# Two heads' compressed probabilities turned in one transpose, placed last in an unbroken run of five

## The chip, the cores and the metric

The kernel runs on one core of a Trainium2 chip. The metric is device time in microseconds (us) from start to end of the program. The core has a matrix engine, TensorE (PE), and four others that work beside it: VectorE (DVE), ScalarE (ACT), GpSimd (POOL), and SyncE (SP), whose queue starts most DMA transfers. Each engine works through its own list of instructions in order and waits on semaphores for the others. Matrix results go to PSUM, in banks of 128 partitions by 512 fp32 columns; operands are read from SBUF.

## The reference

One step of a hybrid decoder layer: a normalised and modulated input, one wide projection, two token mixers (sparse attention and a gated DeltaNet), a merge, an output projection and an MLP. The change touches the sparse attention of the 512 prompt tokens. Its three branches each have their own softmax, and each is scaled by a gate per head before the sum:

```python
s = jnp.einsum('nqghd,ncgd->nqghc', q, kc) * scale
p_cmp = _masked_softmax(s, (kc_end[None, :] <= qp)[None, :, None, None, :])
o_cmp = jnp.einsum('nqghc,ncgd->nqghd', p_cmp, vc)
...
out = gates[..., 0:1] * o_cmp + gates[..., 1:2] * o_slc + gates[..., 2:3] * o_win
```

`kc` and `vc` are keys and values compressed over blocks of tokens; with 512 tokens there are 31 of them, padded to 32. There are 16 query heads in four groups that share keys and values.

## The kernel before

All matrix work in fp32 precision is done as split products: a value is written as a rounded part (hi, type fp32r) and a remainder (lo), and hi x hi, lo x hi and hi x lo are summed in PSUM. So most things that TensorE reads are made by a pair: ACT copies a rounded hi, DVE subtracts it to give lo.

`attention` goes over 32 units (g, i, pr): four groups g, two pairs of heads pr in each, and four blocks of 128 queries i. For each unit `scores` makes probabilities, and `values`, one unit later, multiplies them with the values, so that scores of one unit and values of the one before overlap. In `scores` each of the two heads gets three arrays: `p0` for the 32 compressed keys, `p1` for the selected blocks and `p2` for the window, both 128*(i+1) wide. TensorE makes the scores (tiles `bsp<-K,qst` in the profile), DVE adds the mask and finds the extreme (L1440), ACT takes the exponential and the row sum (L1464), DVE turns sums and gates into one factor per array (L1469 to L1474), and POOL multiplies the six arrays by their factors (L1477), in the order p0, p1, p2 of the first head, then of the second. The two `p0` lie next to each other in one buffer of `pcs` (a part of `consts` in the profile), 64 columns in all.

In `values` probabilities must be turned, so that keys lie on partitions. `tr` (L160) is a TensorE transpose against the identity. The two `p0` are turned first, one after the other, each into 32 partitions of a PSUM bank `pct`; ACT copies them as the rounded part into `st` (L1486, rows 0 to 31) and DVE puts the remainder into rows 32 to 63 (L1487). `st` is the tile `msk`, shown as `rounded`. Then `flipped(j)` turns block j of `p1` and `p2` of both heads, four transposes into a bank `pt`; ACT makes `pth` from it (L1495) and DVE `ptl` (L1496). The products are collected in a bank `po` (`bek` in the profile); the one with the compressed values reads `vcp`, which holds the same 32 rows of compressed values at partitions 0 to 31 and 32 to 63, hi and lo side by side in its columns:

```python
mm(po[:, 0:256], vcp[:, g], st, start=False, stop=False)
```

The banks of `scores`, `pct` and `pt` come from one ring of four PSUM banks (`bsp`).

Around this, `run` weaves the other generators and a stream of projection units together (`bpg` in the profile: eight times three matmuls for each half of the tokens, L153). The Python code keeps an estimate of TensorE's time, `pe_time`, and lets a generator go on when it is due; `yield` names how long it may rest. The emission order and a priority for attention then go to a scheduler that lays down each engine's list. Units of the stream may have a gate; the `ma` units are gated on `split_q`, which attention itself reaches only every fourth unit. A helper, `quarters`, already had the form that the change takes over: first instruction at normal priority, the following ones at priority 20000 and kept in program order, so that they stand together.

Of the kernel before, what the change touches and what calls it, by code (L numbers as in the profile page):

```python
# [11 lines left out]
ALU = mybir.AluOpType  # L12
# [44 lines left out]
def f32(x):  # L57
    return x.bitcast(F32)
# [11 lines left out]
def hybrid_step(ctx: ExitStack, tc: tile.TileContext, A, O, dbg=None):  # L70


    nc = tc.nc
# [27 lines left out]
    def t2(name, dt=F32):  # L101
        return wk.tile([128, SLOT], dt, name=name, tag="t2k")
# [14 lines left out]
    def cst(shape, dt):  # L117

        n = 1
        for v in shape[1:]:  # L120
            n *= v
        r = dt == F32R
        x = (rounded if r else consts)[0:shape[0], cused[r]:cused[r] + n]
        cused[r] += -(-n // 8) * 8
        assert cused[r] <= (CW, CR)[r]
        x = x.bitcast(dt) if dt == I32 else x
        return x if len(shape) == 2 else x.rearrange("p (a b) -> p a b", a=shape[1])
# [12 lines left out]
    def bank(tag):  # L140
        tag = "sp" if tag in ("sc", "pt") else tag
        return ps.tile([128, 512], F32, name="b" + tag, tag=tag, bufs=4 if tag == "sp" else 2)
# [7 lines left out]
    pe_time = [0.0]  # L150
# [8 lines left out]
    def tr(out, in_, idn):  # L159
        nc.tensor.transpose(out, in_, idn)  # L160
        pe_time[0] += 0.107
# [17 lines left out]
    for hf in range(2):  # L179
        c = slice(hf * 512, hf * 512 + 512)  # L180
# [32 lines left out]
    ident = cst([128, 128], F32)  # L213
# [15 lines left out]
    pc = bank("pt")  # L229
# [1193 lines left out]
    def scores(g, i, pr):  # L1423
        n = 128 * (i + 1)
        cs = slice(i * 128, (i + 1) * 128)
        mk, mc = slot["mk"], slot["mc"]
        mx = wk.tile([128, 6], F32, name="mx", tag="sm6", bufs=12)
        sm = wk.tile([128, 6], F32, name="sm", tag="sm6", bufs=12)
        pcs.append(pcs.pop(0))
        pc = pcs[-1]  # L1430
        pp = []

        def score(q, K, c0, c1):
            p = bank("sc")
            mm(p[:, 0:c1 - c0], q[0][:, cs], K[:, g, c0:c1], start=True, stop=False)
            mm(p[:, 0:c1 - c0], q[1][:, cs], K[:, g, c0:c1], start=False, stop=True)
            return p

        def maskmin(out, p, m, acc, init=3.0e38):
            nc.vector.tensor_tensor_reduce(out=out, in0=p, in1=m, scale=1.0, scalar=init, op0=ALU.add, op1=ALU.min, accum_out=acc)  # L1440

        for a_ in range(2):
            ql = qst[2 * g + pr][a_]
            a = a_ * 3
            p0 = pc[:, a_]
            x = t2("ps")
            p1, p2 = x[:, 0:n], x[:, n:2 * n] if i < 2 else t2("pw")[:, 0:n]
            if i < 3:
                pb = score(ql, slot["Ks"], 0, 32 + n)
                maskmin(p0, pb[:, 0:32], mc[:, i], mx[:, a:a + 1])  # L1450
                maskmin(p1, pb[:, 32:32 + n], mk[:, 512 - n:512], mx[:, a + 1:a + 2])
            else:
                pb = score(ql, slot["Ks"], 0, 288)
                maskmin(p0, pb[:, 0:32], mc[:, i], mx[:, a:a + 1])
                maskmin(p1[:, 0:256], pb[:, 32:288], mk[:, 0:256], mx[:, a + 1:a + 2])
                yield 0.3 * YA
                pb = score(ql, slot["Ks"], 288, 544)
                maskmin(p1[:, 256:512], pb[:, 0:256], mk[:, 256:512], mx[:, a + 1:a + 2], mx[:, a + 1:a + 2])
            yield 0.3 * YA
            pd = score(ql, slot["Kw"], 0, n)  # L1460
            maskmin(p2, pd[:, 0:n], mk[:, 512 - n:512], mx[:, a + 2:a + 3])
            parts = (p0, p1, p2)
            for b_, x in enumerate(parts):
                nc.scalar.activation(x, x, AF.Exp, scale=-1.0, bias=mx[:, a + b_:a + b_ + 1],  # L1464
                                     accum_out=sm[:, a + b_:a + b_ + 1])
            pp.append(parts)
            yield 0.5 * YA
        sc = wk.tile([128, 6], F32, name="scl", tag="sm6", bufs=12)
        nc.vector.tensor_scalar(sm, sm, 1.0e-30, None, op0=ALU.max)  # L1469
        nc.vector.reciprocal(sc, sm)  # L1470
        h0 = 16 + (g * 4 + pr * 2) * 3
        nc.vector.tensor_tensor(sc, sc, gtok[:, i, h0:h0 + 6], op=ALU.mult)
        if i == 0:
            nc.vector.tensor_scalar(sc[:, 0:4:3], sc[:, 0:4:3], rv, None, op0=ALU.mult)  # L1474
        for a_ in range(2):
            for b_, x in enumerate(pp[a_]):
                nc.gpsimd.tensor_scalar(x, x, sc[:, a_ * 3 + b_:a_ * 3 + b_ + 1], 1.0, op0=ALU.mult, op1=ALU.mult)  # L1477
        return pp

    def values(g, i, pr, pp):  # L1480
        cs = slice(i * 128, (i + 1) * 128)
        pct = bank("pt")
        for a_ in range(2):
            tr(pct[0:32, a_ * 128:(a_ + 1) * 128], pp[a_][0], ident)
        st = msk.rearrange("p a c -> p (a c)")
        nc.scalar.copy(out=st[0:32], in_=pct[0:32, 0:256])  # L1486
        nc.vector.tensor_tensor(st[32:64], pct[0:32, 0:256], f32(st[0:32]), op=ALU.subtract)  # L1487

        def flipped(j):
            pt = bank("pt")  # L1490
            for b_ in range(2):
                for a_ in range(2):
                    tr(pt[:, (b_ * 2 + a_) * 128:(b_ * 2 + a_ + 1) * 128], pp[a_][1 + b_][:, j * 128:(j + 1) * 128], ident)
            hi, lo = t2("pth", F32R)[:, 0:512], t2("ptl", F32R)[:, 0:512]
            nc.scalar.copy(out=hi, in_=pt)  # L1495
            nc.vector.tensor_tensor(lo, pt, f32(hi), op=ALU.subtract)  # L1496
            return hi, lo
        ptt = flipped(0)
        yield 1 * YA
        po = bank("ek")  # L1500
        for j in range(i + 1):
            for n in range(4):
                mm(po[:, 0:256], slot["V2"][:, n // 2, j, g], ptt[n % 2][:, (n // 2) * 256:(n // 2) * 256 + 256],
                   start=(n + j == 0), stop=(n == 3 and j == i))
                if n + j == 0:
                    mm(po[:, 0:256], vcp[:, g], st, start=False, stop=False)
            if j < i:
                ptt = flipped(j + 1)
                yield 1 * YA
        tm = pp[0][1][:, 0:128]  # L1510
        for a_ in range(2):
            r = slice(a_ * 64, a_ * 64 + 64)
            nc.scalar.copy(out=tm[r], in_=po[64:128, a_ * 128:(a_ + 1) * 128])
            nc.vector.tensor_tensor(tm[r], po[0:64, a_ * 128:(a_ + 1) * 128], tm[r], op=ALU.add)
        t = tma[:, g * 2 + pr, cs]
        nc.vector.scalar_tensor_tensor(t, t, 1.0, tm, op0=ALU.add, op1=ALU.mult)
# [483 lines left out]
```

## Time and profile before

| what | value |
|---|---|
| timed runs | 1309.7, 1305.91 and 1313.38 us, median 1309.7 |
| the profiled execution | 1307.84 us |
| its span, first to last instruction | 1306.1 us |
| mean granted TensorE clock | 0.969 of full |
| busy: PE, DVE, ACT, POOL | 1216.6, 843.8, 647.2, 230.1 us |
| first and last copy of line L1486 | 523.2 and 876.2 us |

Busy time counts instructions that run; matmuls overlap their neighbours, so that the time from one start to the next is less than the duration of one. The granted clock is the share of full speed that TensorE was allowed. The chain of work is followed back from the last instruction to whatever released each step. A wait is put down to the semaphore that came last.

### The profile page before, as it was taken

Reading aid. Unit: us, or ns where it says so; the run is one execution under the profiler, and the core shown is the slowest. Engines: PE = TensorE matmul, PEld = TensorE weight load, DVE = VectorE, ACT = ScalarE, POOL = GpSimd, SP = SyncE. Lnnn points to the kernel's source line nnn. Section 1 sums busy time; section 2 is a strip of 40 time slices with the busy share of each in tenths; the row PEclk is TensorE's granted clock in tenths of the full one; section 3 lists DMA queues with packets and bytes.
Section 4 is the critical chain, followed back from the end, with each engine's and each line's share of the span. In section 5 each row is a group of like instructions: output and inputs, shape, how many; then the busy total and the mean of one; then the engine's idle time right before and its main releaser. Section 6 shows DMA issues by size and latency. Waiting matters only on the chain. (4 is left out here: it accounts for less than half of the span.)

```text
span 1306.1 us, 26716 instructions
## 1 busy us (share of the span) xinstructions
PE 1216.6 (93%) x10356; PEld 1150.1 (88%) x10356; DVE 843.8 (65%) x2291; ACT 647.2 (50%) x1561; POOL 230.1 (18%) x323
## 2 busy tenths in 40 slices
PE   4899899999888999799998899999999999999997
PEld 3788889989788999678887798989999999999996
DVE  4576958795357788787777787896834334334355
ACT  4565857654243336656646677574643132232244
POOL 2112100112111111312221323230431021020000
PEclk9899989999699999899999899999999999999999
DMA  8852412425613345346344222371732332332533
GB/s 273 216 156 74 126 32 51 119 78 151 182 47 108 103 130 146 98 116 197 99 116 136 74 72 85 94 196 33 210 95 69 98 95 83 97 97 83 161 90 105
DMA packets 234834, 149.82 MB, mean 115 GB/s; under 512 B 9290, under 2 KB 230018, under 8 KB 234444
## 3 DMA queue, kind: packets, MB, share of 16 engines
q1 hardware_dynamic: 224804, 134.77, 36.4%
q0 software_dynamic: 2240, 6.38, 1.8%
q10 hardware_dynamic: 7664, 6.97, 1.8%
q8 instruction: 81, 1.33, 0.4%
q14 instruction: 45, 0.37, 0.1%
HBM read 136.87 MB, written 15.60 MB: 117 GB/s over the span
## 5 line engine op out<-in xcount | busy, mean ns | idle before, releaser
L153 PE MATMUL bpg<-hh,wh 128*128 128x256 f32 (+1 forms) x1168 | 342.2, 293 | 1.2 <-ACT hh L1521 0.7
L153 PE MATMUL bpg<-hh,wl 128*128 128x256 f32 (+1 forms) x1168 | 337.5, 289 | 2.0 <-DVE wl L401 2.0
L153 PE MATMUL bpg<-hl,wh 128*128 128x256 f32 (+1 forms) x1168 | 337.7, 289 | 0.0
L153 PEld LDWEIGHTS bpg<-hh,wh 128*128 128x128 f32 x1168 | 225.2, 193 | 5.2 <-issue 2.0
L153 PEld LDWEIGHTS bpg<-hh,wl 128*128 128x128 f32 x1168 | 224.5, 192 | 4.0 <-DVE wl L401 2.5
L153 PEld LDWEIGHTS bpg<-hl,wh 128*128 128x128 f32 x1168 | 225.5, 193 | 1.5 <-issue 0.8
L401 DVE TENSOR_TENSOR wl<-raw,wh 128x1024 fp32r<-128x1024 f32 x149 | 183.0, 1229 | 65.7 <-ACT wh L397 60.3
L397 ACT CAST wh<-raw 128x1024 fp32r<-128x1024 f32 x117 | 121.6, 1048 | 181.9 <-PE bpg L153 174.5
L153 PE MATMUL bpg<-act,wh 128*128 128x264 f32 (+1 forms) x1024 | 186.5, 284 | 0.0
L153 PEld LDWEIGHTS bpg<-act,wh 128*128 128x128 f32 x1024 | 157.7, 188 | 0.1
L153 PE MATMUL bpg<-act,wl 128*128 128x264 f32 (+1 forms) x512 | 145.0, 284 | 0.2 <-DVE wl L401 0.2
L153 PE MATMUL bpg<-h2h,wh 128*128 128x256 f32 (+1 forms) x448 | 126.7, 283 | 0.0
L153 PE MATMUL bpg<-h2h,wl 128*128 128x256 f32 (+1 forms) x448 | 126.6, 282 | 0.0
L153 PE MATMUL bpg<-h2l,wh 128*128 128x256 f32 (+1 forms) x448 | 126.3, 282 | 0.0
L1848 POOL TENSOR_TENSOR r<-r 128x520 f32<-128x520 f32 (+2 forms) x40 | 54.1, 1354 | 291.2 <-ACT r L1847 291.2
L1811 DVE SCALAR_TENSOR_TENSOR o_dn<-bpg,consts,o_dn 128x256 f32<-128x256 f32 x80 | 38.3, 484 | 100.3 <-PE bpg L153 100.3
L153 PEld LDWEIGHTS bpg<-act,wl 128*128 128x128 f32 x512 | 96.5, 189 | 0.5 <-DVE wl L401 0.4
L153 PEld LDWEIGHTS bpg<-h2h,wl 128*128 128x128 f32 x448 | 84.4, 188 | 0.3 <-DVE wl L401 0.2
L153 PEld LDWEIGHTS bpg<-h2l,wh 128*128 128x128 f32 x448 | 84.4, 188 | 0.0
L153 PEld LDWEIGHTS bpg<-h2h,wh 128*128 128x128 f32 x448 | 84.3, 188 | 0.0
L153 PE MATMUL bsp<-K,qst 128*128 128x288 f32 (+6 forms) x288 | 68.9, 317 | 5.5 <-DVE consts L267 2.3
L1851 DVE TENSOR_TENSOR act<-r,act 128x520 fp32r<-128x520 f32 (+2 forms) x40 | 23.6, 590 | 73.4 <-ACT act L1850 73.3
(634 smaller groups left out, 2453.3 us busy)
## 6 DMA issues: line engine op xcount, KB each, us to landing
raw<-in_w_in SPq DMA_DIRECT2D x68, 512.0 KB
wa<-in_w_ada SPq DMA_DIRECT2D x48, 512.0 KB
raw<-in_w_down SPq DMA_DIRECT2D x40, 512.0 KB
raw<-in_w_up SPq DMA_DIRECT2D x36, 512.0 KB
raw<-in_w_out SPq DMA_DIRECT2D x12, 512.0 KB
Sx<-in_state_dn SPq DMA_DIRECT2D x16, 256.0 KB
out_s_dn<-Sx SPq DMA_DIRECT2D x16, 256.0 KB
pg<-in_cache_k_slc SPq DMA_DIRECT2D x16, 128.0 KB
```

The source lines that it names most:

```text
L153: nc.tensor.matmul(out, lhs, rhs, start=start, stop=stop)
L397: nc.scalar.copy(out=wh, in_=raw)
L401: nc.vector.tensor_tensor(wl[:, 0:kp], raw[:, 0:kp], f32(wh[:, 0:kp]), op=ALU.subtract)
L1811: nc.vector.scalar_tensor_tensor(xi[:, q], p[:, 0:n], mod[:, m + i, 0:1], xi[:, q], op0=ALU.mult, op1=ALU.add)
L1848: nc.gpsimd.tensor_tensor(r, r, r, op=ALU.mult)
L1851: nc.vector.tensor_tensor(b_, r, f32(a), op=ALU.subtract)
```

## The change

The two compressed blocks of a unit are no longer turned one by one. `scores` hands over the 64 columns that hold both, and one transpose turns them into 64 partitions, head 0 in rows 0 to 31 and head 1 in rows 32 to 63. Since the two heads now lie on different partitions, the rounded copy and the subtraction are done once per head, 32 rows by 128 columns each. For head 1 hi and lo change places in `st` (hi in rows 32 to 63, lo in 0 to 31), which `vcp` allows, since its two halves are equal.

The transposes also get a new order. Block 0 is turned first, beginning with the window part of the second head, which POOL scales last; the other three follow at high priority and in program order, and the compressed transpose comes after them as the fifth. For the following blocks the four stand together in the same way. On ACT and DVE the copies of the compressed part come after `pth` and `ptl`.

```diff
         for a_ in range(2):
             for b_, x in enumerate(pp[a_]):
                 nc.gpsimd.tensor_scalar(x, x, sc[:, a_ * 3 + b_:a_ * 3 + b_ + 1], 1.0, op0=ALU.mult, op1=ALU.mult)
+        pp.append(pc.rearrange("p a c -> p (a c)"))
         return pp
 
     def values(g, i, pr, pp):
         cs = slice(i * 128, (i + 1) * 128)
-        pct = bank("pt")
-        for a_ in range(2):
-            tr(pct[0:32, a_ * 128:(a_ + 1) * 128], pp[a_][0], ident)
         st = msk.rearrange("p a c -> p (a c)")
-        nc.scalar.copy(out=st[0:32], in_=pct[0:32, 0:256])
-        nc.vector.tensor_tensor(st[32:64], pct[0:32, 0:256], f32(st[0:32]), op=ALU.subtract)
+        lo_hi = (slice(0, 32), slice(32, 64))
+
+        def turn(out, in_, first):
+            with nullcontext() if first else tc.high_priority(20000):
+                r = nc.tensor.transpose(out, in_, ident)
+            if not first:
+                tc.keep_in_program_order(r)
+            pe_time[0] += 0.107
 
         def flipped(j):
             pt = bank("pt")
-            for b_ in range(2):
-                for a_ in range(2):
-                    tr(pt[:, (b_ * 2 + a_) * 128:(b_ * 2 + a_ + 1) * 128], pp[a_][1 + b_][:, j * 128:(j + 1) * 128], ident)
+            for a_ in (1, 0):
+                for b_ in (1, 0):
+                    turn(pt[:, (b_ * 2 + a_) * 128:(b_ * 2 + a_ + 1) * 128], pp[a_][1 + b_][:, j * 128:(j + 1) * 128], a_ + b_ == 2)
+            if j == 0:
+                pct = bank("pt")
+                turn(pct[0:64, 0:128], pp[2], False)
             hi, lo = t2("pth", F32R)[:, 0:512], t2("ptl", F32R)[:, 0:512]
             nc.scalar.copy(out=hi, in_=pt)
             nc.vector.tensor_tensor(lo, pt, f32(hi), op=ALU.subtract)
+            if j == 0:
+                for a_ in range(2):
+                    c = slice(a_ * 128, (a_ + 1) * 128)
+                    nc.scalar.copy(out=st[lo_hi[a_], c], in_=pct[lo_hi[a_], 0:128])
+                    nc.vector.tensor_tensor(st[lo_hi[1 - a_], c], pct[lo_hi[a_], 0:128], f32(st[lo_hi[a_], c]), op=ALU.subtract)
             return hi, lo
         ptt = flipped(0)
```

The lists below name tiles as the profile does: `bsp<-consts 32x128` and `bsp<-consts 64x128` are the compressed transposes before and now, `bsp<-consts,ps` and `bsp<-consts,pw` those of `p1` and `p2`, `bek<-pth`, `bek<-ptl` and `bek<-rounded` the products with the values, `bsp<-K,qst` scores. L160 and L153 are helpers; in the changed kernel the transposes of `values` have line L1488. TensorE's list has 384 of these transposes in 86 groups before and 352 in 70 groups now.

TensorE's list before, at the end of the third of the four stretches in which projection matmuls are missing (731 to 747 us of the trace):

```order
L153 MATMUL bek<-ptl,V_5790 128x256
L160 MATMUL bsp<-consts 32x128
L160 MATMUL bsp<-consts,ps 128x128 x3
L160 MATMUL bsp<-consts 32x128
L160 MATMUL bsp<-consts,ps 128x128 x2
L160 MATMUL bsp<-consts,pw 128x128 x2
L160 MATMUL bsp<-consts,ps 128x128
L160 MATMUL bsp<-consts,pw 128x128 x4
```

The same place now:

```order
L153 MATMUL bek<-ptl,V_5790 128x256
L1488 MATMUL bsp<-consts,pw 128x128
L1488 MATMUL bsp<-consts,ps 128x128
L1488 MATMUL bsp<-consts,pw 128x128
L1488 MATMUL bsp<-consts,ps 128x128
L1488 MATMUL bsp<-consts 64x128
L1488 MATMUL bsp<-consts,pw 128x128
L1488 MATMUL bsp<-consts,ps 128x128
```

The compressed transposes stood between the others, each where its head's arrays are; now one of them ends the run of block 0.

ACT's list before, at the first call of `values` (L1387 belongs to the sample's DeltaNet):

```order
L1464 ACTIVATE ps,sm<-ps,mx 128x128
L1486 CAST rounded<-bsp 32x256
L1464 ACTIVATE consts,sm<-consts,mx 128x32
L1464 ACTIVATE ps,sm<-ps,mx 128x128 x2
L1495 CAST pth<-bsp 128x512
L1387 CAST rounded<-bsp 8x128
```

And now:

```order
L1464 ACTIVATE ps,sm<-ps,mx 128x128
L1464 ACTIVATE consts,sm<-consts,mx 128x32
L1464 ACTIVATE ps,sm<-ps,mx 128x128 x2
L1502 CAST pth<-bsp 128x512
L1507 CAST rounded<-bsp 32x128
L1387 CAST rounded<-bsp 8x128
L1502 CAST pth<-bsp 128x512
L1507 CAST rounded<-bsp 32x128
```

The one copy ahead of `pth` has become two behind it, the second of them behind the next call's `pth`.

TensorE's list before, in the fourth of those stretches (ahead of and in 811 to 819 us; `bek<-consts,ma` belongs to the modulation):

```order
L153 MATMUL bek<-pth,V_5790 128x256
L153 MATMUL bsp<-K,qst 128x416 x2
L153 MATMUL bpg<-hl,wh 128x264
L153 MATMUL bek<-consts,ma 128x9 x2
L153 MATMUL bek<-ptl,V_5790 128x256
L153 MATMUL bek<-pth,V_5790 128x256
L153 MATMUL bek<-ptl,V_5790 128x256
L153 MATMUL bsp<-K,qst 128x384 x2
L153 MATMUL bpg<-hh,wl 128x264
L160 MATMUL bsp<-consts 32x128 x2
```

And now:

```order
L153 MATMUL bek<-pth,V_5790 128x256
L153 MATMUL bsp<-K,qst 128x416 x2
L153 MATMUL bek<-consts,ma 128x9 x2
L153 MATMUL bek<-ptl,V_5790 128x256
L153 MATMUL bek<-pth,V_5790 128x256
L153 MATMUL bek<-ptl,V_5790 128x256
L153 MATMUL bsp<-K,qst 128x384 x2
L1488 MATMUL bsp<-consts,ps 128x128 x4
L1488 MATMUL bsp<-consts 64x128
L153 MATMUL bsp<-K,qst 128x288 x2
```

The projection matmuls (`bpg`) that stood between the pieces of attention here now stand ahead of them.

## Rows read from the trace of the kernel before

**Rows 1.** The page's first part, busy time, share of the span and instructions.
```profile
PE 1216.6 (93%) x10356; PEld 1150.1 (88%) x10356; DVE 843.8 (65%) x2291; ACT 647.2 (50%) x1561; POOL 230.1 (18%) x323
```

**Rows 2.** Windows: length; busy per engine; then granted clock, DMA share, GB/s.
```profile
515.00:900.00 385.00, 355.64 (x2892) 322.04 (x2891) 299.53 (x1018) 239.06 (x713) 98.44 (x198) 0.97 0.39 113
531.00:547.00 16.00, 11.17 (x66) 7.91 (x65) 12.40 (x57) 13.55 (x42) 5.65 (x13) 0.77 0.32 98
687.00:703.00 16.00, 13.11 (x130) 11.24 (x123) 12.54 (x45) 8.80 (x28) 2.52 (x5) 1.00 0.59 182
731.00:747.00 16.00, 10.75 (x52) 8.67 (x52) 9.97 (x41) 12.69 (x39) 5.19 (x11) 0.70 0.33 88
811.00:819.00 8.00, 6.45 (x47) 5.30 (x48) 5.69 (x25) 4.53 (x18) 3.34 (x6) 0.81 0.97 246
```

**Rows 3.** The chain that ended last: start, length, engine, line.
```profile
946.57 303.91 PE bpg L153 x2529
...
1258.02 0.22 PE bsp L160 x2
```

**Rows 4.** Windows of 4 us in the third and the fourth stretch.
```profile
735.00:739.00 4.00, 2.30 (x10) 1.92 (x11) 3.88 (x13) 3.88 (x12) 0.00 (x0) 0.81 0.33 80
739.00:743.00 4.00, 2.34 (x9) 1.36 (x8) 3.58 (x18) 3.88 (x12) 2.25 (x5) 0.50 0.19 56
743.00:747.00 4.00, 3.82 (x17) 3.45 (x18) 1.41 (x6) 3.90 (x13) 2.94 (x7) 0.50 0.00 0
...
815.00:819.00 4.00, 3.17 (x16) 3.01 (x16) 1.78 (x4) 1.29 (x6) 2.88 (x5) 0.62 1.18 288
```

**Rows 5.** Line L160: count, ns min/median/max, first and last start, forms.
```profile
L160 PE MATMUL bsp<-consts,ps x208: 270/273/476, 523.0 to 882.4; 128*128 128x128 f32 x104
...
L160 PE MATMUL bsp<-consts x85: 164/272/396, 89.1 to 874.2; 128*32 128x128 f32 x64, 128*8 128x128 f32 x13, 128*88 128x128 f32 x3, 128*128 128x128 f32 x3
```

**Rows 6.** PE's timeline, a transpose among projection matmuls: start, duration, instruction.
```profile
703.43 0.28 PE L153 MATMUL bpg<-hh,wl 128*128 128x264 f32 x1
703.55 0.27 PE L160 MATMUL bsp<-consts,ps 128*128 128x128 f32 x1
...
703.78 0.28 PE L153 MATMUL bpg<-hl,wh 128*128 128x264 f32 x1
```

**Rows 7.** Windows of line L1486 alone: ACT busy and count.
```profile
531.00:547.00 16.00, 0.72 (x2) 0.77 0.32 98
...
811.00:819.00 8.00, 0.27 (x1) 0.81 0.97 246
```

**Rows 8.** Lines of the copies, columns as in rows 5.
```profile
L1486 ACT CAST rounded<-bsp x32: 344/361/363, 523.2 to 876.2; 32x256 fp32r<-32x256 f32 x32
...
L1487 DVE TENSOR_TENSOR rounded<-bsp,rounded x32: 412/414/415, 524.0 to 878.1; 32x256 fp32r<-32x256 f32 x32
...
L1387 ACT CAST rounded<-bsp x8: 236/248/255, 406.3 to 565.5; 8x128 fp32r<-8x128 f32 x8
...
L1389 DVE TENSOR_TENSOR rounded<-bsp,rounded x8: 279/280/280, 407.4 to 567.0; 8x128 fp32r<-8x128 f32 x8
...
L1495 ACT CAST pth<-bsp x80: 557/586/619, 524.7 to 883.3; 128x512 fp32r<-128x512 f32 x80
```

**Rows 9.** PE's waits from 515 to 900 us: total, times, longest.
```profile
PE bsp L160 <- POOL consts L1477: 4.3, 4, 2.2
...
PE bsp L153 <- DVE rounded L1487: 2.2, 2, 1.4
PE bsp L160 <- POOL ps L1477: 2.0, 4, 0.8
...
PE bsp L160 <- DVE rounded L1487: 0.7, 1, 0.7
```

**Rows 10.** POOL's timeline in the third stretch; in brackets idle before and releaser.
```profile
740.63 0.29 POOL L1477 TENSOR_SCALAR consts<-consts,scl 128x32 f32<-128x32 f32 x1 [11.89 <-DVE mx L1440]
```

**Rows 11.** Window of line L160 alone: PE and weight load busy, then clock, DMA.
```profile
591.00:607.00 16.00, 4.69 (x30) 3.45 (x30) 1.00 0.81 233
```

## The prediction

> **What bounds the kernel now.** I read the page's first part, then the windows, then the chain, then the waits. The page shows TensorE (PE) busy 1216.6 of 1306.1 us and the next engine, VectorE (DVE), 843.8 [rows 1]. PE's missing 89.5 us are what can still be won. The windows give the attention stretch's share of them: from 515 to 900 us PE lacks 385.00 - 355.64 = 29.4 us [rows 2]. From 946.57 us on, the chain that ended last is one unbroken piece of 2529 matmuls, 303.91 us long, 0.12 each [rows 3]. So whatever makes the attention stretch end earlier, or lets more projection work fit into it, reaches the end one for one.
>
> The attention stretch is not of one kind. For most of it projection matmuls (bpg) fill what attention leaves free on PE. In four places PE's list has next to none of them (the code lets some units start only when attention has got far enough): 531 to 547, 687 to 703, 731 to 747 and 811 to 819 us. There PE lacks 4.8, 2.9, 5.3 and 1.6 us, half of the 29.4, and in three of them the granted clock falls, to 0.77, 0.70 and 0.81 of full on average [rows 2]. Between 735 and 743 us DVE and ScalarE (ACT) are busy 3.6 to 3.9 of every 4 us while PE has 2.3 [rows 4]: there attention's own chain sets the pace, and PE's time costs nothing.
>
> **The transpose that goes.** `values` runs 32 times. Before, each call turns two blocks of 32 columns and then four of 128; now it turns one block of 64 and the same four. What is streamed through is 128 columns each time, and narrow and wide turns last the same, median 272 and 273 ns [rows 5]; their spacing counts, not that duration. Two turns take 0.22 us of the chain, 0.11 each [rows 3]. One alone among projection matmuls costs the same: from 703.43 to 703.78 us stand a matmul, a turn and a matmul, 0.35 us [rows 6]; less two steps of 0.12 for the matmuls, 0.11 is left. So putting turns side by side is worth nothing by itself; leaving one out is worth 0.11. The trace has no turn of 64 columns; its neighbours on both sides, 32 and 128, cost alike, so I take the same. That is 32 x 0.11 = 3.5 us of PE work. Six of the 32 calls lie in the four places (two, one, two and one copies of L1486, by the windows of that line; the first and the last stand in [rows 7]), where PE waits anyway. I count 26 x 0.11 = **-2.9 us**, with -3.5 as the bound.
>
> **The copies that are split.** One ACT copy of 32x256 (median 361 ns) and one DVE subtraction of 32x256 (414 ns) become two of 32x128 each. The new form is not in the trace at 32 rows; L1387 and L1389 do the same at 8 rows and 128 columns, in 248 and 280 ns [rows 8], and rows read in parallel should not matter. Per call ACT gets 2 x 248 - 361 = 135 ns more, DVE 2 x 280 - 414 = 146 ns; over 32 calls 4.3 and 4.7 us. A gain is excluded, since half the columns cost more than half the time in both pairs [rows 8]. Where projection matmuls cover, this is hidden: DVE is busy 299.53 of 385 us and ACT 239.06 [rows 2]. In the four places it lies on the path, six times 0.15 for DVE, with ACT's part running beside it: **+0.9 us**. The upper bound, if DVE were on the path throughout, is +4.7.
>
> **The run.** The four turns of block 0 now begin with the operand that GpSimd (POOL) scales last, the other four follow at high priority in a fixed order, and the compressed turn comes last. The list has 352 turns in 70 groups instead of 384 in 86. Nothing is queued behind a new semaphore, but two things move. First, on ACT and DVE the compressed copies now stand behind `pth` and `ptl`. `pth` gains up to 0.36 us where it stood behind L1486; the matmul that reads the compressed part needs its operand later. On PE that matmul stands at least 9 instructions, about 1.1 us, behind its turn. The way it must cover is 0.59 for `pth` [rows 8] and two of 0.25 and one of 0.28 for the compressed copies, 1.4 us: in the two calls with only 9, PE may wait some 0.3 each. I set 0 and keep 0.6 as the bound. Second, PE's waits on POOL become one wait per call. All PE waits that touch this are 4.3 and 2.0 us on POOL and 2.2 and 0.7 us on L1487, which frees the PSUM bank: 9.2 in all [rows 9]. I count nothing of it, because the row shows who was late: at 740.63 us POOL itself had been idle for 11.89 us waiting on DVE [rows 10]. The old turns trickled along behind POOL's products, and block 0 needs the last product in either order. Late next is the same product. DMA queues keep their transfers; they are issued from the same places.
>
> **Sum:** -2.9 + 0.9 = -2.0 us. The profiled execution took 1307.84 us, its span 1306.1 and 1.7 around it; the median of the three timed runs is 1309.7, and all four average 1309.2. I put the change on that average: **1307 us**. Its own range goes from -3.5 with the copies free to -2.9 + 4.7 + 0.6 = +2.4: 1306 to 1312.
>
> [...]
>
> **Rivals.** (1) The waits go. If one wait per call replaces the scattered ones and the lost time was PE's order rather than late data, up to 9.2 us come back on top of 3.5: 1309.2 - 12.7 = 1297 us. For it: PE met POOL or L1487 in 11 waits [rows 9]. Against: the idle POOL of [rows 10]. It counts as faster once 4 of the 9.2 return.
> (2) Slower: attention's chain paces more of the stretch. In PE's list the fourth place has lost the projection matmuls that stood between its pieces of attention. If it turns into a place like the third, PE's loss there grows from 1.6 to 5.3 us, 3.7 more, and the clock's with it: from 739 to 747 us 6.16 us of busy time ran at half clock, 3.1 lost, against (1 - 0.62) x 3.17 = 1.2 in the fourth [rows 4]. With DVE's 4.7 then on the path and PE's saving unused: 3.7 + 1.9 + 4.7 = +10.3, so 1319.5 us. For it: DVE at 3.88 of 4 us in the third place [rows 4]. Against: outside the four places, 329 of the 385 us, projection matmuls are there to fill [rows 2]. It decides from about +7.
> (3) It does not pay at all: the removed turns were all in time that PE has to spare, or the scheduler breaks the run again elsewhere; then +0.9 to 0, 1309 to 1310 us.
> (4) One more clock fall because of the runs: 3.1 us by the half-clock piece above, 1310 us. The three falls in the trace all stand where PE idled, none at a run of turns under matmul cover.
>
> **Chances.** The forecast 0.45, (1) 0.27, (2) 0.17, (3) 0.07, (4) 0.04. A measurement of this kernel can tell about 0.5% from no change, 6.5 us, so the band around 1309.7 is 1303.2 to 1316.2. The forecast, (3) and (4) fall in it: same 0.56; faster 0.27; slower 0.17. The range should leave out no more than a third of (1) and half of (2): 1297 to 1318. Its lower end is the whole of (1); its upper end is a little short of (2).
>
> **What would show it.** PE has 32 transposes fewer, and the compressed turn keeps the width of 0.11 us: if it took more, the first term is wrong. The new copies should last near 0.25 and 0.28 us. Right would be a PE idle sum between 515 and 900 us near 29 us, with the stretch's end some 2 us earlier; (1) would show as the waits on POOL and on the bank shrinking by several us, (2) as a low PE row and a clock near 0.7 in the fourth place, (4) as a clock fall inside a run without idle time ahead of it. I am wrong above all if the scheduler's new order, which differs everywhere after 520 us, moves idle time that has nothing to do with these turns: its 29.4 us are ten times my sum.

## The result: slower by 1.25%, and the profile after

The changed kernel took 1328.62 us (median of four runs, 1327.02 to 1334.32) against 1311.54 for the kernel before beside it; the ratio is 1.0125, with an interval of 1.0093 to 1.0157. The prediction was 1307 us and a range of 1297 to 1318, so the time is outside it, on the side of rival (2) and beyond its 1319.5. The profiled execution took 1329.4 us, span 1327.6.

The page's first part of the changed kernel, which answers to [rows 1]:

```profile
PE 1232.0 (93%) x10324; PEld 1162.4 (88%) x10324; DVE 856.0 (64%) x2323; ACT 654.0 (49%) x1593; POOL 236.6 (18%) x323
```

PE runs 32 instructions fewer, as it should, and yet is busy 15.4 us longer, since at the lower clock a matmul lasts longer (a turn 0.42 us from 716 to 718 us, at a granted clock of 0.51, and 0.27 at 816 us, at 1.00; rows below). The windows of the changed kernel (length; busy of PE, weight load, DVE, ACT, POOL; granted clock, DMA share, GB/s) answer to [rows 2] and [rows 4]:

```profile
515.00:900.00 385.00, 347.25 (x2756) 313.79 (x2755) 304.65 (x1035) 239.70 (x731) 103.54 (x197) 0.94 0.39 112
711.00:715.00 4.00, 1.94 (x17) 1.74 (x15) 3.97 (x17) 3.40 (x13) 4.00 (x5) 1.00 0.02 5
715.00:719.00 4.00, 3.06 (x15) 3.02 (x16) 2.63 (x6) 2.89 (x8) 0.88 (x1) 0.63 0.71 233
791.00:795.00 4.00, 1.06 (x9) 0.85 (x7) 3.52 (x12) 3.89 (x13) 4.00 (x4) 0.94 0.00 0
795.00:799.00 4.00, 3.23 (x15) 3.20 (x16) 2.19 (x8) 3.10 (x10) 2.74 (x7) 0.50 0.43 131
...
827.00:835.00 8.00, 6.05 (x53) 4.77 (x52) 6.76 (x28) 4.86 (x20) 4.19 (x6) 1.00 1.03 254
```

In the same 385 us PE lacks 37.75 us where it lacked 29.4, and the clock is 0.94 where it was 0.97. The four rows of 4 us show the pattern: PE has 1.94 and 1.06 of 4 us while DVE, ACT and POOL are nearly full, and in the next 4 us the granted clock is 0.63 and 0.50. Such falls stand in nine places of the attention stretch now, in three before. The last row is the fourth place of [rows 2], found again by its matmuls of the modulation: there the clock no longer falls.

The chain of the changed kernel (start, length, engine, line) answers to [rows 3]:

```profile
968.16 303.81 PE bpg L153 x2529
```

The end piece is as long as it was, so the loss lies ahead of it. The two profiled executions are 21.5 us apart, the medians 17.1. From the first exponential of attention (506.6 us before, 510.0 now) to this piece 440.0 us have become 458.2, **18.2 us more**; the other 3.4 us lie ahead of attention, where the traces of all runs are up to 11 us apart. Summed over windows of 2 us in that stretch, PE's idle time went from 30.9 to 41.7 us, and what its busy time lost to a lower clock, (1 - granted clock) x busy, from 9.5 to 19.5. These 20.8 us, less 3.5 for the turns, are nearly the whole of the 18.2.

What PE waits for, 515 to 946 us of the changed kernel (total us, times, longest), answers to [rows 9]:

```profile
PE bsp L1488 <- POOL pw L1477: 10.5, 5, 3.7
PE bek L153 <- ACT pth L1502: 4.7, 4, 2.5
PE bek L153 <- DVE rounded L1508: 3.3, 2, 2.2
```

The waits on POOL, 6.3 us before, are 10.5, all on the last product of a unit (before, these waits are the same if the window goes on to 946 us). The last row is new: before, no product of [rows 9] waited for the compressed part itself. The groups of the lines that the change wrote (ns min/median/max, first and last start, forms):

```profile
L1488 PE MATMUL bsp<-consts x32: 270/272/421, 528.2 to 896.3; 128*64 128x128 f32 x32
...
L1502 ACT CAST pth<-bsp x80: 564/587/617, 528.4 to 901.5; 128x512 fp32r<-128x512 f32 x80
...
L1507 ACT CAST rounded<-bsp x64: 238/257/259, 528.9 to 898.8; 32x128 fp32r<-32x128 f32 x64
...
its engine sat idle before it (us, times) until:
  DVE rounded L1508: 7.0, 12
...
L1508 DVE TENSOR_TENSOR rounded<-bsp,rounded x64: 279/281/283, 529.8 to 899.2; 32x128 fp32r<-32x128 f32 x64
```

Every duration is what the neighbours in [rows 5, 8] let expect: 272 ns for the turn, 257 and 281 for the copies. What was not expected is the idle line under L1507: ACT's second copy, which touches other columns than DVE's first subtraction, waits for that subtraction. The wait is one that the program sets: in the trace the second copy waits for the semaphore that DVE's subtraction raises, in all 32 calls. The two share no element of `st`, but both read the bank `pct` and both write the tile `st`; which of the two the wait is for, no run here shows. The four instructions of a call run as a chain from engine to engine: copy, subtraction, copy, subtraction.

One call in the timelines (start, duration, instruction; in brackets idle before and releaser), ACT first, then DVE, then PE:

```profile
747.33 0.59 ACT L1502 CAST pth<-bsp 128x512 fp32r<-128x512 f32 x1
747.81 0.25 ACT L1507 CAST rounded<-bsp 32x128 fp32r<-32x128 f32 x1
...
749.02 0.60 ACT L666 CAST qst<-LU 64x512 fp32r<-64x512 f32 x1
749.64 0.62 ACT L667 CAST qst<-LU 64x512 fp32r<-64x512 f32 x1
750.29 0.26 ACT L1507 CAST rounded<-bsp 32x128 fp32r<-32x128 f32 x1
```

```profile
748.29 0.68 DVE L1503 TENSOR_TENSOR ptl<-bsp,pth 128x512 fp32r<-128x512 f32 x1
749.00 0.28 DVE L1508 TENSOR_TENSOR rounded<-bsp,rounded 32x128 fp32r<-32x128 f32 x1
...
750.43 0.68 DVE L668 TENSOR_TENSOR qst<-LU,qst 64x512 fp32r<-64x512 f32 x1
...
751.56 0.41 DVE L1440 CUSTOM_DVE_ANT_0 ps<-bsp,masks 128x256 f32<-128x256 f32 x1
...
752.01 0.28 DVE L1508 TENSOR_TENSOR rounded<-bsp,rounded 32x128 fp32r<-32x128 f32 x1
```

```profile
748.42 1.73 PE L153 MATMUL bsp<-K,qst 128*128 128x256 f32 x6
752.35 0.58 PE L153 MATMUL bek<-rounded 128*128 128x256 f32 x1 [2.20 <-DVE rounded L1508]
```

Each of the four instructions is short, but between them both engines do other work that their lists put there: ACT from 749.28, when the first subtraction ends, to 750.29, and DVE from 750.55, when the second copy ends, to 752.01 us. From the first copy to the end of the last subtraction it takes 752.29 - 747.81 = 4.5 us, and PE stands for the last 2.2 of them. Of the kernel before, a call in the third stretch:

```profile
736.30 0.36 ACT L1486 CAST rounded<-bsp 32x256 fp32r<-32x256 f32 x1
...
737.42 0.41 DVE L1487 TENSOR_TENSOR rounded<-bsp,rounded 32x256 fp32r<-32x256 f32 x1
```

That is 1.53 us. Below, this time from the start of a call's first copy into `st` to the end of its last subtraction is called the **turn-around**; its median over the 32 calls of a profile (the 16th in order) is 1.28 us before and 3.07 us after.

### The profile page after: what moved, and what is told of

Its sections match the earlier page's. It is cut to its first block, busy times and chain, and to the rows that moved or that the text cites. A ratio compares the mean times of both kernels' runs of the same rounds, so it can differ in the third digit from the quotient of the medians.

```text
span 1327.6 us, 26694 instructions
## 1 busy us (share of the span) xinstructions
PE 1232.0 (93%) x10324; PEld 1162.4 (88%) x10324; DVE 856.0 (64%) x2323; ACT 654.0 (49%) x1593; POOL 236.6 (18%) x323
## 5 line engine op out<-in xcount | busy, mean ns | idle before, releaser
L153 PE MATMUL bpg<-hh,wh 128*128 128x264 f32 (+1 forms) x1168 | 344.3, 295 | 7.3 <-ACT wh L397 2.5
L153 PE MATMUL bpg<-hh,wl 128*128 128x264 f32 (+1 forms) x1168 | 339.7, 291 | 2.0 <-DVE wl L401 2.0
L153 PE MATMUL bpg<-hl,wh 128*128 128x264 f32 (+1 forms) x1168 | 340.3, 291 | 0.0
L153 PEld LDWEIGHTS bpg<-hh,wh 128*128 128x128 f32 x1168 | 227.8, 195 | 12.2 <-ACT LU L700 3.0
L153 PEld LDWEIGHTS bpg<-hh,wl 128*128 128x128 f32 x1168 | 227.6, 195 | 3.4 <-DVE wl L401 2.5
L153 PEld LDWEIGHTS bpg<-hl,wh 128*128 128x128 f32 x1168 | 228.3, 195 | 2.4 <-issue 1.6
L153 PE MATMUL bpg<-act,wh 128*128 128x264 f32 (+1 forms) x1024 | 186.6, 284 | 0.0
L153 PEld LDWEIGHTS bpg<-act,wh 128*128 128x128 f32 x1024 | 157.7, 188 | 0.1
L153 PE MATMUL bpg<-act,wl 128*128 128x264 f32 (+1 forms) x512 | 145.0, 284 | 0.2 <-DVE wl L401 0.2
L153 PE MATMUL bpg<-h2h,wh 128*128 128x256 f32 (+1 forms) x448 | 126.6, 283 | 0.0
L153 PE MATMUL bpg<-h2h,wl 128*128 128x256 f32 (+1 forms) x448 | 126.5, 282 | 0.0
L153 PE MATMUL bpg<-h2l,wh 128*128 128x256 f32 (+1 forms) x448 | 126.3, 282 | 0.0
L153 PEld LDWEIGHTS bpg<-act,wl 128*128 128x128 f32 x512 | 96.5, 189 | 0.5 <-DVE wl L401 0.4
L153 PEld LDWEIGHTS bpg<-h2l,wh 128*128 128x128 f32 x448 | 84.4, 188 | 0.0
L153 PEld LDWEIGHTS bpg<-h2h,wh 128*128 128x128 f32 x448 | 84.4, 188 | 0.0
L153 PEld LDWEIGHTS bpg<-h2h,wl 128*128 128x128 f32 x448 | 84.3, 188 | 0.0
L153 PE MATMUL bsp<-K,qst 128*128 128x288 f32 (+6 forms) x288 | 68.2, 321 | 4.4 <-DVE mx L1440 2.0
```

The costliest lines, as they stand in the source:

```text
L153: nc.tensor.matmul(out, lhs, rhs, start=start, stop=stop)
```

## The experiments

Four theories. **A**: the time that the split adds on DVE and ACT lies on the path. **B**: the scheduler lays TensorE's list anew for any edit, and the list before fits unusually well. **C**: the unbroken run makes PE stand for POOL's last product. **D**: the split copies' chain, not their time, is what costs. Each ratio is to the kernel before, with its 95% interval. The recorded expectations use letters of their own. Up to e13, A there is the run (here C), B the split copies with their number and their chain (here A and D), C the new list (here B), and the D of e5 is the loss of a turn; in e18 and e19, A is the chain (here D) and B the list.

### The parts of the change, each without the others

The two heads merged into one turn, with the split copies, behind block 0, all else as before:

```diff
+        pp.append(pc.rearrange("p a c -> p (a c)"))
...
+        pct = bank("pt")
+        tr(pct[0:64, 0:128], pp[2], ident)
+        for a_ in range(2):
+            c = slice(a_ * 128, (a_ + 1) * 128)
+            nc.scalar.copy(out=st[lo_hi[a_], c], in_=pct[lo_hi[a_], 0:128])
+            nc.vector.tensor_tensor(st[lo_hi[1 - a_], c], pct[lo_hi[a_], 0:128], f32(st[lo_hi[a_], c]), op=ALU.subtract)
```

> The merge alone: one transpose of 64 columns and the split copies, placed behind block 0 as in the changed kernel, but with the old order of the turns and without priority or fixed order. Theory A (the run, started with POOL's last product, makes TensorE stand still for POOL and the clock fall): between -4 and +3 us against before, waits on POOL near 6 us. Theory B (the four copies in a row delay the compressed product): 12 to 18 us slower, with waits on the second subtraction. Theory C (any new order of TensorE's list costs or gains as much): anywhere within 15 us either way.

Measured: 1.0171 [1.0146, 1.0195]. The merge alone is slower than the whole change, and its 22 us are more than any of the three theories had set. The same with the pace of the emission as before (`pe_time[0] += 0.107` behind the turn):

> The merge alone again, with the planner told to count the transpose that is gone, so that the emission order is that of the kernel before. If the shift of the emission order (theory C) made the 22 us of the merge alone: within 8 us of before. If the merge's own work made it (theory B): 15 us or more slower still.

Measured: 1.0159 [1.012, 1.0197]. The pace by itself is not the reason.

The run alone: `turn` and its order as in the change, but two narrow turns into 32 partitions and one undivided copy and subtraction behind `pth` and `ptl`:

```diff
+                for a_ in range(2):
+                    turn(pct[0:32, a_ * 128:(a_ + 1) * 128], pp[a_][0], False)
...
+            if j == 0:
+                nc.scalar.copy(out=st[0:32], in_=pct[0:32, 0:256])
+                nc.vector.tensor_tensor(st[32:64], pct[0:32, 0:256], f32(st[0:32]), op=ALU.subtract)
```

> The run alone: order, priority and place of the turns as in the changed kernel, but two compressed transposes of 32 columns and one copy pair of 256 columns as before. A: 12 to 20 us slower than before, waits on POOL's last product near 10 us and a mean clock near 0.955. B: within 4 us of before. C: anywhere within 15 us.

Measured: 1.0069 [1.0047, 1.0091]. PE's waits from 515 to 946 us there:

```profile
PE bsp L1488 <- POOL pw L1477: 14.4, 7, 4.2
```

So C's wait is real, and larger than after the whole change, but the kernel is faster than that. Its 9.5 us are less than the run theory and more than the copies theory had set; only the bounds of the list theory hold them. The changed kernel with the run begun at POOL's first product:

```diff
-            for a_ in (1, 0):
-                for b_ in (1, 0):
+            for a_ in (0, 1):
+                for b_ in (0, 1):
...
```

> The changed kernel with the run begun at the product that POOL makes first instead of last (the others still follow at once in fixed order). A: the stand moves inside the run but stays, since the run can't be left: 12 to 20 us slower than before, like the changed kernel, with the waits named on several products. B: the same 12 to 18 us slower. C: anywhere within 15 us. If only the reversal were at fault, within 4 us of before.

Measured: 1.0206 [1.0183, 1.0229]. Its waits on POOL from 515 to 946 us are fewer than after the change, 4.2 us against 10.5, and still it is the slowest kernel here:

```profile
PE bsp L1488 <- POOL ps L1477: 2.7, 4, 1.8
PE bsp L1488 <- POOL pw L1477: 1.5, 3, 0.8
```

So nothing is won by trickling along inside a run that may not be broken, and the waits on POOL do not rank the kernels. Whether the order of the run makes the 0.8% between e3 and the changed kernel isn't shown, since lists with equal work lie that far apart too (next section).

### The same work under other lists

The instructions stay as before; what is changed is a number that paces the emission or, in the last, the place of the copies. First one number at which every list came out as before, which shows what the measurement itself does (`pe_time[0] += 0.107` per unit):

> The kernel before with the planner's clock changed the other way: one transpose more counted per unit, no change of work. Theory C (the list before is a lucky or tuned one, and any other costs): 4 to 15 us slower. Otherwise: within 4 us, and the 6 us of the other shift was a single case.

Measured: 0.9982 [0.9957, 1.0007]. Then three where lists differ (`-= 0.107`, `-= 0.214`, `+= 0.3`), one with `yield 1.1 * YA` for `yield 1 * YA`, and one with the copy and subtraction of `st`, undivided, behind `pth` and `ptl`:

> The kernel before with nothing but the planner's clock changed: it counts one transpose fewer per unit, as the changed kernel does, so that the emission order shifts while the work stays. A and B: within 4 us of before. C: a difference of 6 us or more either way would show that the order alone moves the time that far.

> The kernel before, the planner counting two transposes fewer per unit: the same work in another order. Theory C (the order alone makes the loss): 10 us or more slower than before. Theory B (the split copies make most of it): 0 to 8 us slower, like the other change of pace.

> The kernel before, the planner counting 0.3 us more per unit: the same work in another order, which differs from the one before in about as many places as the changed kernel's does. C: 10 us or more slower. B: -4 to 8 us.

> The kernel before with the rest after block 0's transposes a tenth longer in the planner: the same work in another order. C: 10 us or more slower. B: -4 to 8 us.

> The kernel before with its one copy and one subtraction of the compressed part moved behind those of block 0, as the changed kernel has them, but not split; both narrow transposes stay first. If the late place of these copies is what costs: 10 us or more slower. B in its plain form (their number costs): -2 to 8 us, with the compressed product's wait on the subtraction below 2 us.

Measured, in this order: 1.0039 [1.0021, 1.0056], 1.0064 [1.0032, 1.0095], 1.009 [1.006, 1.0121], 1.0059 [1.0038, 1.0079], 0.9982 [0.9963, 1.0002]. B holds in part: four of five new lists for the same work are slower, by 0.4 to 0.9%. In e4 one row of PE's waits shows it:

```profile
PE bsp L160 <- POOL consts L1477: 10.0, 4, 5.3
```

It was 4.3 us [rows 9], with no product and no turn changed. But none of the five reaches 1.0125, though the intervals of e11 and the changed kernel overlap, and copies that merely come later (e13) cost nothing.

### The copies

Only ACT's copy divided by head, only DVE's subtraction, both in turn, and both with the two copies ahead of the two subtractions; the turns as before:

```diff
 e14
+        for c in (slice(0, 128), slice(128, 256)):
+            nc.scalar.copy(out=st[0:32, c], in_=pct[0:32, c])
 e15
+        for c in (slice(0, 128), slice(128, 256)):
+            nc.vector.tensor_tensor(st[32:64, c], pct[0:32, c], f32(st[0:32, c]), op=ALU.subtract)
 e5
+        for a_ in range(2):
+            c = slice(a_ * 128, (a_ + 1) * 128)
+            nc.scalar.copy(out=st[0:32, c], in_=pct[0:32, c])
+            nc.vector.tensor_tensor(st[32:64, c], pct[0:32, c], f32(st[0:32, c]), op=ALU.subtract)
 e16
+        for c in (slice(0, 128), slice(128, 256)):
+            nc.scalar.copy(out=st[0:32, c], in_=pct[0:32, c])
+        for c in (slice(0, 128), slice(128, 256)):
+            nc.vector.tensor_tensor(st[32:64, c], pct[0:32, c], f32(st[0:32, c]), op=ALU.subtract)
```

> The kernel before with only ScalarE's compressed copy split in two; VectorE's subtraction stays whole. Same work in another order costs 0 to 9 us in the runs so far. If ScalarE's part makes the loss of the split: 12 to 18 us slower than before. If VectorE's part does, or the two only together: 0 to 9 us.

> The kernel before with only VectorE's compressed subtraction split in two; ScalarE's copy stays whole. If VectorE's added 4.7 us make the loss of the split: 12 to 18 us slower than before. If ScalarE's part does, or the two only together: 0 to 9 us.

> The kernel before with only the copies of the compressed part split by head: the two transposes of 32 columns stay as they are, ScalarE's one copy of 256 columns becomes two of 128 and VectorE's one subtraction becomes two. No transpose goes, the planner counts as before. Theory B (the split copies are what costs): 8 to 20 us slower than before. Theory A (the run) and theory D (the transpose that went was what the order hung on): within 4 us, since the added 4 to 5 us of ScalarE and VectorE time lie beside projection matmuls.

> Both split, the two narrow transposes kept, but both copies ahead of both subtractions, so that ScalarE's second copy does not wait for VectorE. If the chain copy, subtraction, copy, subtraction made the 16 us of the split alone: 0 to 9 us slower than before. If the number of instructions made it: 12 to 18 us.

Measured: ACT's alone 1.0018 [0.9996, 1.0041], DVE's alone 0.9988 [0.997, 1.0006], both in a chain 1.013 [1.009, 1.017], both in pairs 1.0047 [1.0018, 1.0076]. The group of the subtraction in e15, and those of copy and subtraction in e5:

```profile
L1488 DVE TENSOR_TENSOR rounded<-bsp,rounded x64: 269/279/282, 529.4 to 886.8; 32x128 fp32r<-32x128 f32 x64
```

```profile
L1488 ACT CAST rounded<-bsp x64: 237/254/258, 528.5 to 896.4; 32x128 fp32r<-32x128 f32 x64
...
its engine sat idle before it (us, times) until:
  DVE rounded L1489: 6.1, 6
...
L1489 DVE TENSOR_TENSOR rounded<-bsp,rounded x64: 279/280/282, 529.3 to 897.5; 32x128 fp32r<-32x128 f32 x64
```

A falls as the main cause: e15 has all of DVE's added time and loses nothing, and e16 has the added time of both engines and loses 0.5%, which lies among the lists with equal work. e5 and e16 issue the same instructions on the same operands and differ in the order alone; the chained one is slower by 0.8%, and only in it ACT waits for DVE: the second copy waits for the subtraction's semaphore in all 32 calls of e5 and in none of e16. That could still be B, an unlucky list; so the chain of e5 was put under two more lists, with e12's and with e4's number:

```diff
 e18 = e5 and
-        yield 1 * YA
+        yield 1.1 * YA
 e19 = e5 and
+        pe_time[0] -= 0.107
```

> The kernel of e5 (both copies split by head, in the order copy, subtraction, copy, subtraction) with one number changed that alters no instruction: the rest that values allows itself after block 0 is 1.1 units instead of 1, so that the scheduler lays the lists anew. If the split's chain itself costs about 1% (theory A), this kernel stays near e5: 1.010 to 1.016. If e5 had only met a list that fits badly (theory B), this one falls back among the lists that were laid anew with equal work: 0.999 to 1.008. In the profile theory A shows half-clock time and idle time like e5's (19 and 37 us before the unbroken end piece), theory B less of both.

> The kernel of e5 with another number changed: the estimate of TensorE's time that paces the emission is lowered by 0.107 per unit, as e4 did to the kernel before. A third list for the same split work. Theory A (the chain of copy, subtraction, copy, subtraction costs about 1% under any list): 1.010 to 1.016. Theory B (the list decides): anywhere in 0.998 to 1.009, and apart from e18 by more than their intervals.

Measured: 1.0121 [1.0084, 1.0159] and 1.0129 [1.0085, 1.0173]. All three chained kernels lie within 0.1% of one another. The lists are not wholly independent: by the traces PE's list in e19 is that of e5 up to 670 us and another one from there on; in e18 it differs from 544 us on. Against the unchained kernel with the same number the chain costs 1.3% (e5 to before), 0.6% (e18 to e12) and 0.9% (e19 to e4). The stretch from the first exponential to the unbroken end piece agrees: it is longer by 17, 8.4 and 8.2 us in these three pairs of profiles (in e5 up to the last 2529 matmuls of a piece that is longer there), while in e7, with the lists of the kernel before, it is 439.0 us against 440.0. That is what D says. Its nearest control, the same split in pairs (e16), has been measured under one list only.

Two more start from the changed kernel. One takes the chain away by giving both copies ahead of both subtractions, the other by copying undivided: one copy and one subtraction of 64x128 into rows 0 to 63 and 64 to 127 of `st`, and two products of 128 columns with zero-padded compressed values in place of one of 256.

```diff
 e9
                     nc.scalar.copy(out=st[lo_hi[a_], c], in_=pct[lo_hi[a_], 0:128])
+                for a_ in range(2):
+                    c = slice(a_ * 128, (a_ + 1) * 128)
                     nc.vector.tensor_tensor(st[lo_hi[1 - a_], c], pct[lo_hi[a_], 0:128], f32(st[lo_hi[a_], c]), op=ALU.subtract)
 e17
+                nc.scalar.copy(out=st[0:64], in_=pct[0:64, 0:128])
+                nc.vector.tensor_tensor(st[64:128], pct[0:64, 0:128], f32(st[0:64]), op=ALU.subtract)
...
+                    for a_ in range(2):
+                        mm(po[:, a_ * 128:(a_ + 1) * 128], vcp[a_][:, g], st, start=False, stop=False)
```

> The changed kernel with both rounded copies ahead of both subtractions, so that ScalarE's second copy no longer waits for VectorE's first subtraction; the work is the same. Theory B in its narrow form (the chain copy, subtraction, copy, subtraction is what delays the compressed product): at least half of the loss comes back, 5 to 10 us slower than before. Theories A and C: 12 us slower or more, as the changed kernel.

> The changed kernel with its merge and its run, but with the copies whole: the 64 turned rows are copied by one instruction of 64x128 and subtracted by one of 64x128, the remainder goes to rows 64 to 127, and two products of 128 columns with two masked copies of the compressed values take the place of one of 256. ScalarE and VectorE then have 0.1 us less per unit than before, not 0.14 more. If the split copies are what made the changed kernel slow: as the run alone or better, 0 to 10 us slower than before. If the run or the order made it: 14 us or more slower, as the changed kernel.

Measured: e9 1.0114 [1.0066, 1.0161], e17 1.0081 [1.0051, 1.0112]. e9 doesn't come down as D would have it; the chain theory had set half of the loss or more to come back. The chain is gone there (no second copy waits for DVE's semaphore), but its list has the largest wait on POOL of all kernels, twice that of the changed one:

```profile
PE bsp L1488 <- POOL pw L1477: 20.8, 9, 4.5
```

That this wait took the place of what the chain had cost is argued, not shown: e3 is slower with 4.2 us of such waits. e17's 10.4 us lie at the upper edge of what the chain theory had set for it, 0 to 10.

### All runs side by side

Turn-around as defined above; PE's idle time and what its busy time lost to a lower clock, from the first exponential to the unbroken end piece of the profiled run, in us. L marks the same work under a new list.

| kernel | copies split | turn-around | idle | clock | ratio |
|---|---|---|---|---|---|
| before | no | 1.28 | 30.9 | 9.5 | 1 |
| e13 L | no | 1.38 | 29.3 | 11.1 | 0.998 |
| e15 | DVE only | 1.21 | 30.1 | 12.4 | 0.999 |
| e14 | ACT only | 1.52 | 30.5 | 12.0 | 1.002 |
| e4 L | no | 1.14 | 34.9 | 16.9 | 1.004 |
| e16 | pairs | 1.69 | 33.3 | 13.7 | 1.005 |
| e12 L | no | 1.39 | 32.4 | 14.7 | 1.006 |
| e10 L | no | 1.15 | 36.4 | 15.6 | 1.006 |
| e2 | no | 1.39 | 39.7 | 15.6 | 1.007 |
| e17 | no | 1.39 | 36.0 | 17.4 | 1.008 |
| e11 L | no | 1.78 | 34.1 | 17.0 | 1.009 |
| e9 | pairs | 1.77 | 44.3 | 19.6 | 1.011 |
| e18 | chain | 3.21 | 37.0 | 17.3 | 1.012 |
| after | chain | 3.07 | 41.7 | 19.5 | 1.013 |
| e19 | chain | 3.00 | 38.9 | 18.2 | 1.013 |
| e5 | chain | 3.52 | 37.1 | 19.1 | 1.013 |
| e6 | chain | 3.30 | 42.4 | 16.4 | 1.016 |
| e1 | chain | 3.10 | 46.5 | 21.0 | 1.017 |
| e3 | chain | 3.05 | 48.5 | 26.7 | 1.021 |

The seven chained kernels have a turn-around of 3.0 us and more and a ratio of 1.012 and more; the others stay under 1.8 us and, but for e9, at 1.009 or less. Neighbours in the table have intervals that overlap, so it is the groups that differ, not each pair. No kernel here is faster than the one before by more than its interval.

## Why the prediction was wrong

**The removed turns, -2.9.** Right in count and width: 32 fewer, and a turn of 64 columns starts 0.11 us after the one ahead of it, as the prediction took it:

```profile
816.28 0.27 PE L1488 MATMUL bsp<-consts,ps 128*128 128x128 f32 x1
816.38 0.27 PE L1488 MATMUL bsp<-consts 128*64 128x128 f32 x1
```

No run shows the gain by itself: e17, which keeps it without the chain but adds one product per call, is at 1.0081.

**The split copies, +0.9, at most +4.7.** The price of the instructions was right (257 and 281 ns at 32 rows, [rows 8] gave 248 and 280 at 8), and that their time is hidden was right too for either engine alone, by e14 and e15. The step that failed is the sentence "Nothing is queued behind a new semaphore", with the words "with ACT's part running beside it" and the way of 1.4 us counted for the run: they put the four instructions end to end or side by side. In the changed kernel the second copy waits for a semaphore of DVE in all 32 calls. The four run as a chain, and each link queues behind the other work of its engine, so the way took 3.07 us in the median and 4.5 in the call shown. The 0.6 us bound for `rounded` was 3.3 us in PE's waits alone. By the three chained lists of e5, e18 and e19 against the same numbers without the split, the term should have been +0.6 to +1.3%, some 8 to 17 us, not 0.9 and not the 4.7 of its bound.

**The run, 0.** The reading of [rows 10] held: block 0 needs the last product in either order, and nothing came back. But the waits on POOL grew, from 6.3 to 10.5 us. Whether the run costs anything itself isn't shown: e2's 0.7% lies among the 0.4 to 0.9% of lists with equal work.

**The sum against one trace.** The last sentence of the prediction named the danger, and gave it no price. It has one: a new list with the same work moved this kernel by -0.2 to +0.9%, -2 to +12 us, more than the whole sum. The list of before is at the good end of the six that were seen, so a new one is more likely to lose.

**The rivals.** (2) had the right sign and kind, more stretches in which attention's chain sets the pace and a lower clock with it, 1319.5 us. Its place was wrong: the fourth place has no fall any more, at a clock of 1.00, and of the nine falls only those at 542 and 750 us lie in the four places of the prediction, the other seven where it counted on projection matmuls to cover. Its cause was wrong too, since DVE's 4.7 us are free (e15). (1) is excluded by the grown waits. (3) is excluded by the time. (4) was the author's guess: no row of before shows a fall at a run of turns, and [rows 11] stands at 1.00. The trace of the changed kernel shows no fall without idle time ahead of it: PE had idled for 1.5 to 3.0 of the 4 us before each of the nine, and in the two places above it was busy 1.94 and 1.06 us of 4.

**What stays open.** The way from a long turn-around to the loss is not one row: PE's waits on `rounded` are 3.3 us of 20.8, and in e5 no large one stands. A row that e5, e18 and e19 share, and that the kernel before, e4, e12 and e16 lack, is a wait of transposes and score matmuls for the subtraction of `ptl`, 4.3, 3.8 and 5.1 us in total; of e5:

```profile
PE bsp L153 <- DVE ptl L1498: 3.4, 6, 1.2
...
PE bsp L160 <- DVE ptl L1498: 0.9, 2, 0.5
```

But the changed kernel has only 0.7 us of it and e9, without the chain, 4.0. That later operands and a PSUM bank held longer push the whole unit back, and that idle time then brings the clock down, fits the table but is argued, not shown. How the 1.25% of this very kernel divides between chain and list isn't settled either, because e9, without the chain, is as slow: either its list lost as much, or the chain costs little beside the run.

## What to carry to other kernels

Dividing a copy and a subtraction into two pairs can turn them into a chain across two engines, even where the halves share no element, as here, where the turn-around went from 1.28 to 3.07 us: look at the turn-around, with the queues of both engines in it, not at durations. Keep the pair whole if you can, and look in the lists for a wait that the edit adds. Where a scheduler lays static lists, first measure the same work under a few other lists; a term smaller than their spread, here 1%, can't be forecast from one trace, and the new list is a term of its own.

## What the runs showed of the hardware

Some of POOL's products took far longer than their usual time beside DVE's work, 1.70 us where 0.59 is usual, which the prediction hadn't seen as a cause of the waits on POOL. Of the 32 products of 128x384 in the changed kernel's trace, 17 overlapped by no more than 0.04 us with a TENSOR_TENSOR operation of DVE on two SBUF operands and not at all with a DVE copy from SBUF to SBUF, and all 17 took 0.58 or 0.59 us; the eleven that overlapped such a TENSOR_TENSOR operation by 0.3 us or more took 1.55 in the median, two of them 0.59 and the longest 2.61. The changed kernel's timelines of POOL, of DVE and of PE, ahead of the fall at 716 us:

```profile
711.46 0.59 POOL L1477 TENSOR_SCALAR pw<-pw,scl 128x384 f32<-128x384 f32 x1
712.03 0.82 POOL L1477 TENSOR_SCALAR consts<-consts,scl 128x32 f32<-128x32 f32 x1
712.83 1.38 POOL L1477 TENSOR_SCALAR ps<-ps,scl 128x384 f32<-128x384 f32 x1
714.18 1.70 POOL L1477 TENSOR_SCALAR pw<-pw,scl 128x384 f32<-128x384 f32 x1
```

```profile
713.07 0.68 DVE L399 CAST wh<-raw 128x1024 fp32r<-128x1024 f32 x1
...
714.22 1.20 DVE L401 TENSOR_TENSOR wl<-raw,wh 128x1024 fp32r<-128x1024 f32 x1
```

```profile
715.94 0.43 PE L1488 MATMUL bsp<-consts,pw 128*128 128x128 f32 x1 [3.00 <-POOL pw L1477]
716.16 0.42 PE L1488 MATMUL bsp<-consts,ps 128*128 128x128 f32 x1
```

The same product of 128x384 takes 0.59 us at 711.46 and 1.70 at 714.18, 1.11 more, while DVE subtracts two SBUF operands for 1.20 us; PE stands 3.00 us for its end, and then turns at a spacing of 0.22 us, twice the 0.11 of the turns at 816 us, under the lower clock (0.51 from 716 to 718 us, 1.00 from 815 to 819). By the records the product starts 0.04 us ahead of the subtraction. That DVE's operation is what made the product longer is read from these overlaps and from the size, 1.11 beside 1.20 us; no run here took the operation away to show it.
